# Static engine order in the attention, mixer operands split before DRAM, and PSUM sums in the FFN products of a hybrid block on one core

## The chip, the cores and the metric

The kernel runs on one core of one Trainium2 chip. The metric is the device time of one execution in microseconds (us). TensorE (PE) does the matmuls, VectorE (DVE) and ScalarE (ACT) everything on elements, GpSimd (POOL) a few memsets, and SyncE (SP) issues all DMAs, from one queue, in order.

## The reference, cut to what matters

One layer with 1024 tokens, 1024 channels, hidden width 2816, float32 throughout:

```python
u = modulate(rmsnorm(h, g_ff1), sh1, sc1)
h = h + 0.5 * gt1 * swiglu(u, w1_gate, w1_up, w1_down)
u = modulate(rmsnorm(h, g_mix), sh2, sc2)
qa, ka, va, xm, o_pre, ga, gb = split(u @ w_in)
ya = diff_attention(qa, ka, va, lam, g_subln)      # 8 heads x 2 score maps, chunk-causal
yb = mlstm_branch(xm, o_pre, ...)                  # conv, 4 heads, gated scan over chunks
h = h + gt2 * ((sigmoid(ga) * (ya @ w_proj_a) + sigmoid(gb) * (yb @ w_proj_b)) @ w_out)
u = modulate(rmsnorm(h, g_ff2), sh3, sc3)
h = h + 0.5 * gt3 * swiglu(u, w2_gate, w2_up, w2_down)
out = rmsnorm(h, g_final)
```

The modulation vectors come from `silu(c) @ w_ada + b_ada`, nine blocks of 1024 columns. In the attention every block of 128 queries has two softmaxes over its keys, whose difference multiplies v.

## The kernel before

**Precision.** A float32 product is made of three TensorE passes over rounded halves: operand = high part (`hi`, type fp32r) + low part (`lo`, the rest), and `mm3` (L130) does hi x hi, hi x lo, lo x hi into one PSUM bank (L132, L133, L134). So every operand is split once: a copy to `hi` on ACT and a subtraction to `lo` on DVE (`unit` L121 for weights, `split` L135, and `split_in` L140 for what has been loaded into the place of its low part).

**Stages, in order of time.** The first FFN (`ffn`), whose gate/up part does 3 hidden tiles plainly and 19 in steps of `gate_up`, then its down part; `stage_in`, which projects xm and the output gate, does the causal conv and the gate pre-activations; `stage_mlstm`; `stage_attn`; the merge; the second FFN; the final norm. The hidden layers and what the mixers read pass through DRAM.

**FFN.** `gate_up` (L385) uses one level of Strassen's scheme in Winograd's form: seven products instead of eight for a gate tile and an up tile, each product 4 x 3 matmuls of 128x512 into a PSUM bank of its own (`product`, 8 banks in the ring `psg`). One ACT copy and seven DVE additions then build the four outputs, and DVE also makes the weight combinations s1 to s4 (L391 to L397).

**stage_in.** `conv` (L728) copies the projection of channel tile j to `xp`, makes the conv in `acc` (L738, L741), Silu (L743), and splits both into the four tiles `xh` (one buffer each), which the tiny gate matmuls `gps` (L754, L756) read. It stores `acc` (L746) and `xp` (L747) to DRAM. The gate matmuls of tile j stand four projections later in TensorE's order; so the split of tile j+1 waits for the gate matmuls of tile j. Meanwhile `ada` (L114, L115) takes the columns of `w_ada` for later modulation vectors one by one: a 512 KB load, a multiply-and-sum on DVE.

**Sequence mixers.** mLSTM and attention are short dependent chains; dense projections (`job_qk`, `job_v`, `job_g`, `job_b`, cut into pieces of six matmuls by `chunk` L1003) fill TensorE between their steps. For attention, a head's block pair j does four score blocks (`sc`, L1276/L1277), softmax on DVE and ACT (L1278 to L1291), then for each pair of key blocks a turn (`pt`, four transposes, L1305; one buffer), its split into `ah` (ACT, L137) and `al` (DVE, L138), and the value products (`po`); at a head's end, the norm (`oss`, L1345).

**What orders the work.** TensorE's order is the source order, throughout (`manual_schedule(engines={PE})`, L1433). In the mixers `paced` (L1013) sorts items (due time, cost, function) by due times that `stage_attn` works out from fixed fractions of a block's length, and puts dense pieces between them. ACT and DVE are ordered by a scheduler with priorities; the items of `paced` get a head start of a fixed offset over the dense work's evictions:

```python
for due, cost, fn in sorted(items, key=lambda x: x[0]):
    while now < due:
        c = self.chunk()
        now = now + c if c else due
    with self.tc.high_priority(offset=self.ahead):
        fn()
```

A head's q and k are loaded from DRAM as one float32 tensor (`load`, L1240), then split: `Kh` on ACT (L143), `Kl` on DVE (L144), and for `Q`, whose low part lies on the upper 64 partitions, in four pieces. v is loaded and split the same way (`load_v`).

Of the kernel before, what the change touches and what calls it, by code (L numbers as in the profile page):

```python
# [15 lines left out]
PE = mybir.EngineType.PE  # L16
LNEXP = "natural_log_exp_and_others"
# [3 lines left out]
P = 128  # L21
# [18 lines left out]
class Halves:  # L40
    """two tiles with half of the tokens each"""
# [8 lines left out]

class Net:
    def __init__(self, ctx, tc, aps, dbg):
# [8 lines left out]
        self.uid = 0  # L61
        c = self.const
# [29 lines left out]
    # conditioning: one column block of w_ada per call  # L92
# [27 lines left out]
    # weights  # L120
# [9 lines left out]
    def mm3(self, ps, w, x, start, stop):  # L130
        nc = self.nc
        nc.tensor.matmul(ps, w[0], x[0], start=start, stop=False)  # L132
        nc.tensor.matmul(ps, w[0], x[1], start=False, stop=False)  # L133
        nc.tensor.matmul(ps, w[1], x[0], start=False, stop=stop)  # L134
# [22 lines left out]
    def rstd_of(self, ps, n, last):  # L157
        """1 / sqrt(ps / n + eps); `last`: the activation before it"""
# [9 lines left out]
    # 1 / rms over channels, on every partition, for some of the tokens  # L168
# [35 lines left out]
    def sum_square(self, n, i, m):  # L204
        """add channel tile m of half n, its i-th, to the running sum of squares"""
# [18 lines left out]
    def norm_step(self, i, q, j, bank):  # L224
        """first half's modulation behind the steps of the last products"""
# [8 lines left out]
    def norm_behind(self, i, n, m, bank):  # L234
        """behind the update of channel tile m of half n: statistics, and the first half's modulation"""
# [12 lines left out]
    def group(self, srcs, psp, tag, hook):  # L248
        """several M-tiles of a projection of u at once, channel tile by channel tile"""
# [15 lines left out]
    def ffn(self, wgu, wd, gt, first, plain, hid, after, step, extra=None):  # L265
        """h += gate * (silu(u w_gate) * (u w_up)) w_down; hidden passes through DRAM"""
# [33 lines left out]
    # The hidden layer goes to DRAM as the operands that down() takes: even tiles are its rows b1., odd ones b2.  # L300
# [9 lines left out]
    def store_right(self, hid, f, c2):  # L310
        """what follows from the second token half of tile f"""
# [8 lines left out]
    def store_left(self, hid, f, c1):  # L320
        """what follows from the first token half, behind store_right"""
# [10 lines left out]
    # One level of Strassen's scheme in Winograd's form: 7 products for the 8 of two tiles of w^T u, with  # L332
    # w^T = [a11 a12; a21 a22] (tiles x channel halves) and u = [b11 b12; b21 b22] (channel x token halves)
# [10 lines left out]
    def combine_u(self, x, pool):  # L344
        """t1 = b12 - b11, t2 = b22 - t1, -t4 = b21 - t2 for one channel tile of each half"""
# [26 lines left out]
    def gate_up(self, src, psg, rp, hid, f, first):  # L372
# [24 lines left out]
        A["s4"], A["s3"], A["a22"] = op(a12), op(s3), op(a22)  # L397
# [5 lines left out]
        def product(a, b):  # L403
            ps = psg.tile([P, NW], F32, name=self.nm("gu"), tag="gu")
            (h, l), u = A[a], B[b]
            for x in range(4):
                xs = slice(x * P, x * P + P)
                self.mm3(ps, (h[:, xs], l[:, xs]), u[x], x == 0, x == 3)
            return ps

        def plus(a, b):
            t = self.t512()
            add(t, a, b)
            return t

        m1 = self.t512()
        nc.scalar.copy(m1, product("a11", "b11"))
        c11 = plus(m1, product("a12", "b21"))
        if first:
            for x in range(4):  # L420
                self.combine_u3(x)
        nc.scalar.activation(c11, c11, AF.Silu)
# [4 lines left out]
        nc.scalar.activation(c12, c12, AF.Silu)  # L427
        m7 = product("s3", "t3")
        add(u4, u4, m7)
        nc.vector.tensor_mul(c12, c12, u4)  # L430
        self.store_right(hid, f, c12)
        add(m1, m1, m7)
        add(m1, m1, product("a22", "t4"))
        nc.vector.tensor_mul(c11, c11, m1)
        self.store_left(hid, f, c11)
# [66 lines left out]
        # product: its operands, weights to fetch meanwhile, a combination that takes a weight's place  # L502
# [43 lines left out]
    def first_start(self, srcs, psg, gtag, psd, dtag):  # L546
        """the first block's input: statistics, modulation and the first tiles as x and w_ada come in"""
# [42 lines left out]
    def first_norm(self, i, srcs, psg, gtag, psd, dtag):  # L590
        """later blocks' input: the first tiles run on one half while the other is normalised"""
# [8 lines left out]
    def out_tail(self, n, i, m, bank):  # L600
        """final norm behind the last update of h"""
# [36 lines left out]
    # one M-tile of a projection of u: PSUM halves  # L638
# [18 lines left out]
    def mix_setup(self):  # L657
# [8 lines left out]
        self.xcd, self.xmd, self.od, self.ybd = ([sc(f"{c}{h}", [P, 2, T]) for h in range(4)]  # L666
# [915 lines left out]
```

## Time and profile before

| | |
|---|---|
| median of 3 runs | 2679.71 us (2675.5 to 2680.58) |
| span of the profiled execution | 2681.1 us; the page gives no other time of it |
| TensorE busy | 2592.6 us, 97% |
| VectorE busy | 1877.3 us, 70% |
| ScalarE busy | 1288.3 us, 48% |
| DMA moved | 380.47 MB, mean 142 GB/s |

Stages by the profile: start 0 to 75 us, first FFN gate/up 75 to 467, its down part 467 to 694, `stage_in` 694 to 895, mLSTM 895 to 1211, attention and the dense work left after it 1211 to 1848, merge 1848 to 2035, second FFN 2035 to 2668, last norm and stores to 2681.

How to read it: busy times are instruction spans. Matmuls overlap, so a 128x512 matmul shows some 390 ns though one starts every 0.227 us (391.23 us for 1725 of them in the first gate/up part). PEclk is the clock that TensorE was granted, 1.00 for its higher level (2.4 GHz), 0.50 for the lower (1.2 GHz).

### The profile page before, as it was taken

What the parts mean: (1) busy time and instruction counts of PE and PEld (TensorE: products, weight loads), DVE (VectorE), ACT (ScalarE), POOL (GpSimd) and SP (SyncE); (2) the same over time, 40 slices, a digit from 0 to 9 for tenths busy, and PEclk for the clock granted to TensorE, in tenths of its full rate; (3) what the DMA queues carried; (4) which work ended last, traced back from release to release, by engine and by line L of the source; (5) the groups of instructions that cost most, each with busy time, mean ns of one, the idle gap of its engine ahead of it and who ended that gap; (6) DMA issues with size and microseconds to landing.
All of it is one profiled execution on the core that took longest, in us unless ns stands there. A gap on an engine that the chain in (4) does not pass through costs nothing.

```text
span 2681.1 us, 35203 instructions
## 1 busy us (share of the span) xinstructions
PE 2592.6 (97%) x12704; PEld 2155.8 (80%) x12704; DVE 1877.3 (70%) x3352; ACT 1288.3 (48%) x2369; POOL 22.5 (1%) x85
## 2 busy tenths in 40 slices
PE   6999999999899999999999999999999999999998
PEld 4888887778777799997777778777887888888886
DVE  7987878678795456646766766654467776766867
ACT  6333333446435366654666766753345332323444
POOL 0000000000000000000000000000000000000000
PEclk8999999999999999999999999999999999999999
DMA  7434345833674423334333333558342333236533
GB/s 262 162 130 145 118 149 185 274 99 104 215 258 149 140 91 118 111 100 121 111 102 106 99 105 115 159 198 277 131 140 87 110 98 115 99 102 216 161 95 122
DMA packets 174471, 380.47 MB, mean 142 GB/s; under 512 B 18405, under 2 KB 47529, under 8 KB 174297
## 3 DMA queue, kind: packets, MB, share of 16 engines
q1 hardware_dynamic: 174296, 378.24, 43.6%
q8 instruction: 99, 1.62, 0.2%
q14 instruction: 76, 0.61, 0.1%
HBM read 280.27 MB, written 97.90 MB: 141 GB/s over the span
## 4 chain that ended last, share of the span: by engine, by line
PE 84%; DMA 7%; DVE 5%; ACT 3%; issue 1%; SPq 0%; DVEq 0%; ACTq 0%; POOL 0%; POOLq 0%
PE gu L134 10%; PE gu L133 10%; PE gu L132 10%; PE acc L132 5%; PE acc L133 5%; PE acc L134 5%; PE ab L132 2%; PE ab L133 2%; PE ab L134 2%; PE dn L134 2%; PE dn L132 2%; PE dn L133 2%; PE gp L132 2%; PE gp L134 2%; PE gp L133 2%; PE pt L1305 1%
## 5 line engine op out<-in xcount | busy, mean ns | idle before, releaser
L132 PE MATMUL gu<-uh,wh 128*128 128x512 f32 x800 | 314.2, 393 | 10.1 <-ACT uh L201 8.8
L133 PE MATMUL gu<-ul,wh 128*128 128x512 f32 x800 | 313.4, 392 | 1.3 <-DVE ul L202 1.3
L134 PE MATMUL gu<-uh,wl 128*128 128x512 f32 x800 | 313.2, 391 | 0.8 <-DVE wl L127 0.7
L137 ACT CAST wh<-wr 128x512 fp32r<-128x512 f32 x228 | 134.0, 619 | 253.0 <-PE gu L133 194.0
L132 PE MATMUL acc<-uh,wh 128*128 128x512 f32 x616 | 241.9, 393 | 1.3 <-ACT uh L137 1.3
L133 PE MATMUL acc<-ul,wh 128*128 128x512 f32 x616 | 240.3, 390 | 1.3 <-DVE ul L138 1.3
L134 PE MATMUL acc<-uh,wl 128*128 128x512 f32 x616 | 239.8, 389 | 0.0
L126 ACT CAST wh<-wr 128x1024 fp32r<-128x1024 f32 x120 | 125.8, 1049 | 148.0 <-PE wo L133 46.1
L127 DVE TENSOR_TENSOR wl<-wr,wh 128x1024 fp32r<-128x1024 f32 x120 | 146.5, 1221 | 71.8 <-ACT wh L126 70.9
L132 PEld LDWEIGHTS gu<-uh,wh 128*128 128x128 f32 x800 | 151.2, 189 | 44.3 <-ACT uh L201 10.4
L133 PEld LDWEIGHTS gu<-ul,wh 128*128 128x128 f32 x800 | 151.2, 189 | 34.4 <-DVE ul L202 2.3
L134 PEld LDWEIGHTS gu<-uh,wl 128*128 128x128 f32 x800 | 151.1, 189 | 33.4 <-DVE wl L127 2.3
L133 PE MATMUL gu<-ut,wh 128*128 128x512 f32 x456 | 177.5, 389 | 0.0
L132 PE MATMUL gu<-ut,wh 128*128 128x512 f32 x456 | 177.4, 389 | 0.0
L134 PE MATMUL gu<-ut,wl 128*128 128x512 f32 x456 | 177.4, 389 | 0.0
L138 DVE TENSOR_TENSOR wl<-wr,wh 128x512 fp32r<-128x512 f32 x228 | 152.8, 685 | 1.6 <-ACT wh L137 1.6
L137 ACT CAST uh<-hr 128x512 fp32r<-128x512 f32 x154 | 95.4, 619 | 100.2 <-PE acc L134 63.6
L132 PEld LDWEIGHTS acc<-uh,wh 128*128 128x128 f32 x616 | 115.6, 188 | 28.6 <-ACT uh L137 2.5
L133 PEld LDWEIGHTS acc<-ul,wh 128*128 128x128 f32 x616 | 115.6, 188 | 26.3 <-DVE ul L138 2.2
L134 PEld LDWEIGHTS acc<-uh,wl 128*128 128x128 f32 x616 | 115.6, 188 | 24.1
L138 DVE TENSOR_TENSOR ul<-hr,uh 128x512 fp32r<-128x512 f32 x154 | 105.8, 687 | 35.5 <-ACT uh L137 35.0
L1281 ACT ACTIVATE p<-sc,lr 128x256 f32<-128x256 f32 (+7 forms) x128 | 94.8, 741 | 74.0 <-DVE lr L1279 72.1
(335 smaller groups left out, 6561.4 us busy)
## 6 DMA issues: line engine op xcount, KB each, us to landing
ada<-wada SPq DMA_DIRECT2D x72, 512.0 KB
wr<-win SPq DMA_DIRECT2D x48, 512.0 KB
wr<-w1gu SPq DMA_DIRECT2D x44, 512.0 KB
wr<-w2gu SPq DMA_DIRECT2D x44, 512.0 KB
wr<-wab SPq DMA_DIRECT2D x32, 512.0 KB
g<-t SPq DMA_DIRECT2D x32, 256.0 KB
t<-g SPq DMA_DIRECT2D x32, 256.0 KB
wr<-wout SPq DMA_DIRECT2D x16, 512.0 KB
```

The source lines that it names most:

```text
L126: nc.scalar.copy(hi, raw)
L127: nc.vector.tensor_sub(lo, raw, hi.bitcast(F32))
L132: nc.tensor.matmul(ps, w[0], x[0], start=start, stop=False)
L133: nc.tensor.matmul(ps, w[0], x[1], start=False, stop=False)
L134: nc.tensor.matmul(ps, w[1], x[0], start=False, stop=stop)
L137: (eng or self.nc.scalar).copy(hi, src)
L138: self.nc.vector.tensor_sub(lo, src, hi.bitcast(F32))
L1281: nc.scalar.activation(pc[c][:, 0:W], ps[:, 0:W], AF.Exp, bias=lr[:, 2 + c:3 + c], accum_out=lr[:, c:c + 1])
L1305: nc.tensor.transpose(pt[:, kk, i], a[i][:, kb * P:kb * P + P], self.ident)
```

## The change

No matmul is added or removed. Four parts:

1. **Attention order.** A class `Flow` takes the place of `paced` in `stage_attn`. Scores, values, outputs and loads of a head are generators that yield steps (engine, cost, function), take and give tokens for buffers, and wait for flags. `Flow.run` keeps a clock: a TensorE step that is ready is emitted, otherwise a piece of dense work. Inside it `manual_schedule(engines={PE, ACT, DVE})` holds, so ACT and DVE follow the source order as well. Weights of the dense work are fetched and split one job ahead (`unit_ahead`), evictions of dense banks are put into the model at a delay (`defer`). `p0` gets 6 buffers (was 4), `lr` 6 (was 4), `whl` 4 (was 3); `keep` goes from 90 to 45.
2. **Operands split before DRAM.** q, k, v, xc and xm are written as a high and a low tensor each and loaded as they are; the splits after the loads go, splits ahead of the stores come (in `rotate`, `job_v`), and for xc and xm the tiles `xh` themselves are stored.
3. **FFN sums in PSUM** (`seven`): x = a11*b11, copied by ACT, then s2*t2 and s3*t3 accumulate in the same bank, each copied by ACT; y = s1*t1, read by a DVE addition, then s4*b22 accumulates in it. Four banks instead of seven for a step, four DVE additions instead of seven, three ACT copies instead of one. The order of the seven products changes.
4. `dynamic_dma_scratch_size=1024` is passed at the build.

```diff
+class Flow:
+    LAT, MARGIN = 0.15, 0.4
...
+    def run(self):
+        while self.live:
+            while self.heap and self.heap[0][0] <= self.now:
...
+                    fn()
+                    self.free[eng] = max(self.free[eng], t) + cost
+                    self.push(self.free[eng] + self.LAT, gen)
+            if self.pe:
+                gen, _, cost, fn = self.pe.pop(0)
+                fn()
+                self.now += cost
+                self.push(self.now + self.LAT, gen)
+                continue
+            c = self.chunk()
...
-        self.whl = e(tc.tile_pool(name="whl", bufs=3))
+        self.whl = e(tc.tile_pool(name="whl", bufs=4))
...
-        m1 = self.t512()
-        nc.scalar.copy(m1, product("a11", "b11"))
-        c11 = plus(m1, product("a12", "b21"))
...
-        add(m1, m1, product("s2", "t2"))
-        u4 = plus(m1, product("s1", "t1"))
-        c12 = self.hidden_tile(f, 1)
-        add(c12, u4, product("s4", "b22"))
...
-        m7 = product("s3", "t3")
-        add(u4, u4, m7)
...
-        add(m1, m1, m7)
-        add(m1, m1, product("a22", "t4"))
+        x = product("a11", "b11")
+        c11 = kept(x)
+        add(c11, c11, product("a12", "b21"))
...
+        u2 = kept(product("s2", "t2", x))
+        y = product("s1", "t1")
+        u3 = kept(product("s3", "t3", x))
+        c22 = self.t512()
+        add(c22, u3, y)
+        out(1, 1, c22)
+        z = product("a22", "t4")
+        product("s4", "b22", y)
+        c12 = place() if place else self.t512()
+        add(c12, u2, y)
...
             nc.sync.dma_start(out=self.xcd[j // 2][:, j % 2], in_=acc)
-            nc.sync.dma_start(out=self.xmd[j // 2][:, j % 2], in_=xp[:, 4:4 + T])
+            for p in range(2):
+                nc.sync.dma_start(out=self.xcs[j // 2][p][:, j % 2], in_=xh[p].bitcast(F32))
+                nc.sync.dma_start(out=self.xms[j // 2][p][:, j % 2], in_=xh[2 + p].bitcast(F32))
...
+            for r in range(2):
+                rows = slice(64 * r, 64 * r + 64)
+                for dst, o in ((qs, src[0][r]), (kh, src[1][0]), (kl, src[1][1])):
+                    nc.sync.dma_start(out=dst[rows, :, part].bitcast(F32), in_=o)
...
+            with tc.manual_schedule(engines={PE, ACT, DVE}):
+                self.flow = flow
+                flow.run()
+                self.flow = None
```

`kept(ps)` copies a bank to a tile on ACT; `out` applies Silu or multiplies and stores. (`add` and `sub` are DVE operations.)

**DVE in the attention, around a turn of the first head**: `al` is the low part of a turn, `lr` the row maxima, and `t`/`qa` (after: `ro`) the rotation of a dense projection's result. Before:

```order
L1278 MEMSET sc_12290 64x64
L1279 TENSOR_REDUCE lr_12289<-sc_12290 128x1
L938 TENSOR_TENSOR t_12306<-qa_12179,cos 128x512
L939 TENSOR_TENSOR t_12307<-t_12305,sin 128x512
L941 TENSOR_TENSOR qa_12179<-qa_12179,sin 128x512
L940 TENSOR_TENSOR t_12306<-t_12306,t_12307 128x512
L1278 MEMSET sc_12324 64x64
L942 TENSOR_TENSOR t_12305<-t_12305,cos 128x512
L1279 TENSOR_REDUCE lr_12289<-sc_12324 128x1
L138 TENSOR_TENSOR al_12344<-pt_12338,ah_12343 128x512
```

And in the change, at the first head's second turn:

```order
L1118 TENSOR_TENSOR ro_12179<-ro_12179,ro_12176 128x512
L1119 TENSOR_TENSOR ro_12177<-ro_12177,ro_12178 128x512
L1112 TENSOR_TENSOR ro_12229<-qa_12124,cos 128x512
L1566 TENSOR_TENSOR al_12268<-pt_12237,ah_12256 128x512
L1501 MEMSET sc_12263 64x64
L1502 TENSOR_REDUCE lr_12233<-sc_12263 128x1
L1113 TENSOR_TENSOR ro_12230<-ro_12228,sin 128x512
L1121 TENSOR_TENSOR ro_12179<-ro_12179,ro_12180 128x512
```

Before, `al` stands behind the rotation's operations and the maximum of a later score block; in the change it stands ahead of that block's memset and maximum.

**DVE at the start of stage_in**: `wl` is the low part of the weight of the fourth xm projection, `ada` a column block of `w_ada`, `acc` the conv of the first tile. Before:

```order
L115 SCALAR_TENSOR_TENSOR ada_7128,mod_94<-ada_7128,crep_6282 128x1024
L117 TENSOR_TENSOR mod_94<-mod_94,vec 128x1
L115 SCALAR_TENSOR_TENSOR ada_7132,mod_94<-ada_7132,crep_6282 128x1024
L117 TENSOR_TENSOR mod_94<-mod_94,vec 128x1
L115 SCALAR_TENSOR_TENSOR ada_7136,mod_94<-ada_7136,crep_6282 128x1024
L127 TENSOR_TENSOR wl_6347<-wr_6344,wh_6346 128x1024
L738 TENSOR_SCALAR acc_6292<-xp_6284,vec 128x1024
```

And in the change, where the next eight `ada` (L213) follow only later:

```order
L225 TENSOR_TENSOR wl_6022<-wr_6019,wh_6021 128x1024
L332 TENSOR_TENSOR t_5994<-t_5981,t_5994 128x512
L225 TENSOR_TENSOR wl_6323<-wr_6320,wh_6322 128x1024
L320 TENSOR_TENSOR t_6073<-h_391,t_6060 128x512
L320 TENSOR_TENSOR t_6078<-h_392,t_6060 128x512
```

The fourth `wl` moves from behind the `ada` operations to right behind the third one.

**SP later in stage_in, its DMAs for channel tiles 4 to 6**: `xc`, `xm` and their `h` and `l` forms are stores, `wr` and `ada` loads, each of 512 KB. Before:

```order
L747 DMA xm_307<-xp_6484 128x1024
L114 DMA ada_7297<-wada 128x1024
L114 DMA ada_7362<-wada 128x1024
L746 DMA xc_303<-acc_6492 128x1024
L114 DMA ada_7367<-wada 128x1024
L124 DMA wr_7148<-win 128x1024
L114 DMA ada_7372<-wada 128x1024
L747 DMA xm_307<-xp_6568 128x1024
```

And in the change:

```order
L890 DMA xc_303<-acc_6558 128x1024
L212 DMA ada_7273<-wada 128x1024
L892 DMA xch_317<-xh_6465 128x1024
L893 DMA xmh_325<-xh_6467 128x1024
L892 DMA xcl_318<-xh_6466 128x1024
L893 DMA xml_326<-xh_6468 128x1024
L892 DMA xch_317<-xh_6552 128x1024
L893 DMA xmh_325<-xh_6554 128x1024
L892 DMA xcl_318<-xh_6553 128x1024
L893 DMA xml_326<-xh_6555 128x1024
L890 DMA xc_304<-acc_6645 128x1024
```

One store `xm` gives way to four stores of the tiles `xh`; the `ada` loads between them become few.

## Rows read from the trace of the kernel before

**Rows 1.** The page: span, and the chain that ended last by engine.

```profile
span 2681.1 us, 35203 instructions
...
PE 84%; DMA 7%; DVE 5%; ACT 3%; issue 1%; SPq 0%; DVEq 0%; ACTq 0%; POOL 0%; POOLq 0%
```

**Rows 2.** Stretches: length, busy us (instructions) by engine, PEclk, DMA share, GB/s.

```profile
75.00:467.00 392.00, 391.23 (x1725) 323.30 (x1724) 321.84 (x555) 125.56 (x212) 0.00 (x0) 1.00 0.44 146
694.00:895.00 201.00, 193.66 (x834) 151.64 (x834) 132.99 (x247) 85.02 (x110) 1.10 (x12) 0.98 0.55 190
895.00:1211.00 316.00, 306.17 (x2378) 293.09 (x2378) 184.01 (x469) 191.47 (x549) 13.94 (x32) 1.00 0.36 114
1211.00:1848.00 637.00, 604.87 (x3018) 498.90 (x3016) 418.33 (x770) 400.60 (x715) 6.49 (x32) 0.99 0.44 135
2035.00:2453.00 418.00, 417.63 (x1843) 345.49 (x1842) 306.10 (x491) 141.33 (x236) 0.00 (x0) 1.00 0.33 108
```

**Rows 3.** PE's waits, 1211 to 1848: total us, times, longest us; eleven rows.

```profile
PE pt L1305 <- DVE al L138: 9.2, 9, 2.2
PE sc L1277 <- DVE Kl L144: 3.1, 7, 0.7
PE sc L1276 <- DVE Q L144: 2.5, 1, 2.5
PE po L133 <- DVE al L138: 2.2, 3, 1.8
PE sc L1276 <- ACT Kh L143: 2.0, 4, 1.1
...
PE oss L1345 <- ACT t L1338: 0.6, 1, 0.6
```

**Rows 4.** The timeline around one such wait: start us, duration us, then [idle before].

```profile
1256.30 0.58 ACT L137 CAST ah<-pt 128x512 fp32r<-128x512 f32 x1
...
1259.17 0.67 DVE L138 TENSOR_TENSOR al<-pt,ah 128x512 fp32r<-128x512 f32 x1
1259.90 0.66 PE L1305 MATMUL pt<-ident,p 128*128 128x128 f32 x4 [1.40 <-DVE al L138]
```

**Rows 5.** Stretches at the lower clock, columns as in rows 2.

```profile
733.40:740.20 6.80, 4.79 (x11) 3.80 (x12) 6.80 (x8) 0.00 (x0) 0.00 (x0) 0.50 0.86 278
1453.60:1460.40 6.80, 5.47 (x15) 4.54 (x16) 5.39 (x11) 3.31 (x8) 0.00 (x0) 0.50 0.44 94
1566.30:1569.70 3.40, 3.36 (x11) 2.98 (x12) 3.14 (x6) 1.15 (x3) 0.00 (x0) 0.50 0.47 154
1747.20:1750.60 3.40, 3.40 (x9) 2.63 (x8) 2.85 (x6) 2.75 (x6) 0.00 (x0) 0.50 0.69 239
1846.20:1853.00 6.80, 4.37 (x10) 3.47 (x11) 5.84 (x9) 4.17 (x7) 0.00 (x0) 0.50 0.90 299
```

**Rows 6.** stage_in: PE's wait in 726 to 742, and DVE's timeline ahead of it.

```profile
PE dn L134 <- DVE wl L127: 5.4, 1, 5.4
...
732.98 1.23 DVE L115 SCALAR_TENSOR_TENSOR ada<-ada,crep 128x1024 f32<-128x1024 f32 x1 [1.87 <-DMA ada<-wada]
734.13 1.22 DVE L127 TENSOR_TENSOR wl<-wr,wh 128x1024 fp32r<-128x1024 f32 x1
```

**Rows 7.** stage_in: gate matmuls of tiles 3 to 7 (first and last start), and splits.

```profile
L754 PE MATMUL gps<-xh,G x20: 388/397/398, 797.4 to 828.3; 128*16 128x512 f32 x20
...
L138 DVE TENSOR_TENSOR xh<-xp,xh 128x1024 fp32r<-128x1024 f32 x8 | 9.8, 1220 | 0.0
```

**Rows 8.** Waits, columns as in rows 3: PE in the mLSTM, DVE in 2035 to 2453.

```profile
PE vps L1084 <- DVE mv L138: 3.3, 3, 1.8
...
DVE wr L391 <- DMA wr<-w2gu: 24.8, 17, 2.0
```

**Rows 9.** First gate/up part, by line: busy us, mean ns; idle time before and its releaser.

```profile
L413 DVE TENSOR_TENSOR t<-t,gu 128x512 f32<-128x512 f32 x38 | 26.0, 684 | 23.1 <-PE gu L134 14.7 <-issue 8.4
L417 ACT COPY t<-gu 128x512 f32<-128x512 f32 x19 | 11.2, 588 | 30.9 <-PE gu L134 30.9
```

More of the change, by code (lines that the diff above doesn't have):

```diff
@@ L1 @@
+import heapq
 from contextlib import ExitStack
@@ L16 @@
 PE = mybir.EngineType.PE
+DVE = mybir.EngineType.DVE
+ACT = mybir.EngineType.Activation
 LNEXP = "natural_log_exp_and_others"
@@ L370, in combine_u3, with seven @@
         self.split(t, *self.u_quarter(x, 0, 1))
-    def gate_up(self, src, psg, rp, hid, f, first):
+    def seven(self, src, bank, rp, out, first=False, place=None):
         nc = self.nc
@@ L401, in gate_up, with product @@
         B["t3"] = [self.u_quarter(x, 0, 1) for x in range(4)]
-        def product(a, b):
-            ps = psg.tile([P, NW], F32, name=self.nm("gu"), tag="gu")
+        def product(a, b, ps=None):
+            begin = ps is None
+            if begin:
+                ps = bank()
             (h, l), u = A[a], B[b]
@@ new lines, in load_v, with loads, sc_time @@
+                heads[hd] = v
+            def loads(hd):
+                if hd:
+                    yield "need", ("scored", hd - 1)
+                load(hd, slice(0, 256))
+                load(hd, slice(256, T))
+                yield "wait", 3.5
+                yield "set", ("qk", hd)
+                if hd:
+                    yield "need", ("valued", hd - 1)
+                load_v(hd)
+                yield "wait", 3.5
+                yield "set", ("v", hd)
+            def sc_time(W):
+                return sum(2 * {512: 0.227, 384: 0.174, 256: 0.12, 128: 0.112}[min(NW, W - o)] for o in range(0, W, NW))
@@ L1273, in item, with score, dots @@
+            def score(hd, j, i, c, a):
+                qb = 2 * j + i
+                W = qb * P + P
+                yield "need", ("qk", hd)
+                if hd or j or i or c:
+                    yield "need", ("begun", *self.prev[hd, j, i, c])
+                yield "take", "sc"
+                yield "set", ("begun", hd, j, i, c)
+                x = {}
+                def dots():
+                    x["ps"] = ps = psA.tile([P, T], F32, name=self.nm("sc"), tag="sc")
                     for o in range(0, W, NW):
@@ new lines, in score, with values, turn, high @@
+                yield "give", "p1"
+                yield "set", ("p", hd, j, i)
+            def values(hd, j, a):
+                nk = 2 * j + 2
+                if hd or j:
+                    yield "need", ("turned", *((hd, j - 1) if j else (hd - 1, 3)))
+                for i in range(2):
+                    yield "need", ("p", hd, j, i)
+                parts = {}
+                flow.spawn(flow.now, outputs(hd, j, parts))
+                for kp in range(nk // 2):
+                    yield "take", "pt"
+                    yield "take", "ah"
+                    x = {}
+                    def turn():
+                        x["pt"] = pt = psT.tile([P, 2, 2, P], F32, name=self.nm("pt"), tag="pt")
+                        for kk in range(2):
+                            for i in range(2):
+                                kb = 2 * kp + kk
+                                nc.tensor.transpose(pt[:, kk, i], a[i][0][:, kb * P:kb * P + P], self.ident)
+                    def high():
+                        x["h"] = a2.tile([P, 2, 256], F32R, name=self.nm("ah"), tag="ah")
+                        nc.scalar.copy(x["h"].rearrange("p k q -> p (k q)"), x["pt"].rearrange("p k i q -> p (k i q)"))
+                    def low():
+                        l = a2.tile([P, 2, 256], F32R, name=self.nm("al"), tag="al")
+                        nc.vector.tensor_sub(l.rearrange("p k q -> p (k q)"), x["pt"].rearrange("p k i q -> p (k i q)"),
+                                             x["h"].rearrange("p k q -> p (k q)").bitcast(F32))
+                        parts[kp] = x["h"], l
+                    yield "P", 0.44, turn
+                    if kp == nk // 2 - 1:
+                        yield "give", "p0"
+                        yield "give", "p0"
+                        yield "set", ("turned", hd, j)
+                    yield "A", 0.6, high
+                    yield "D", 0.69, low
+                    yield "give", "pt"
+                    yield "set", ("part", hd, j, kp)
@@ L1355, in stage_attn @@
+            own = lambda j: 2 * (sc_time(2 * j * P + P) + sc_time(2 * j * P + 2 * P)) + (j + 1) * (0.44 + 0.72)
+            items = [(hd, j, i, c) for hd in range(8) for j in range(4) for i in range(2) for c in range(2)]
+            self.prev = {b: a for a, b in zip(items, items[1:])}
+            t = 0.0
             for hd in range(8):
+                flow.spawn(0.0, loads(hd))
                 for j in range(4):
-                    a = [None, None]
-                    length = 4 * score_cost(j) + sum(c for c, _ in late) + dense / 32.0
@@ L1378, in stage_attn @@
-            for x, (cost, f) in enumerate(late):
-                put(off + 2.0 * x, cost, f)
-            put(off + 2.0 * len(late), 0.0, sq)
-            for x, (cost, f) in enumerate(norms):
-                put(off + 2.0 * len(late) + 3.0 * (x + 1), cost, f)
-            self.paced(items)
+                    a = {}
+                    length = own(j) + 0.43 + dense / 32.0
+                    for x in range(4):
+                        flow.spawn(t + x * length / 4, score(hd, j, x // 2, x % 2, a))
```

514 lines of the change are left out of this document (319 added, 195 removed).

## The prediction, as it was put on record

> **What bounds the kernel now.** I read the page first, for the span and the chain that ended last [rows 1]: 84% of 2681.1 us lies on TensorE. Then the stretches of the stages [rows 2], where the reader is to compare the length with PE's busy time: the gate/up parts leave 0.8 us of 392 and 0.4 us of 418, `stage_in` 7.3 of 201, the mLSTM 9.8 of 316, the attention with what follows it 32.1 of 637. Third, PE's waits there [rows 3]: eleven rows from 9.2 to 0.6 us, 26.7 in sum (most of the other 5.4 us lies at the end, ahead of the merge). Fourth, the clock: single stretches at 0.50 [rows 5], each behind a wait of about 2 us or more. Work done in 6.8 us at half clock takes 3.4 at full, so such a stretch costs half its length.
>
> So the kernel is as long as its matmuls, which the change leaves alone, and can only lose waits and lower clock. DVE or ACT work that goes is worth nothing where PE does not wait for it.
>
> **1. The order in the attention.** Of the 26.7 us, 9.2 are turns that wait for the `al` of the turn before, and 2.2 value products that wait for their own [rows 3]. The timeline shows why [rows 4]: `ah` ends at 1256.88, `al` (0.67 us) starts at 1259.17, because DVE does rotation work and a row maximum first; PE stands still for 1.40 us. The change puts `al` ahead of them, and in its TensorE order only one of the close pairs of turns (one dense piece, six matmuls, 1.36 us between them) is left of ten. A turn, `ah` and `al` need about 0.6 + 0.58 + 0.67 us and hand-overs. I take 9.5 of the 11.4 us as gone.
>
> `Kl`, `Kh` and `Q` cost 3.1, 2.0 and 2.5 us [rows 3]. Their splits go, but the loads stay: a head's keys have one buffer, so the loads still stand behind the last score of the head before, now with two tensors of k. I leave 0.3 us for each of seven heads and take 5.5 of 7.6 us as gone.
>
> The other six rows, 26.7 - 11.4 - 7.6 = 7.7 us, are softmax, norm and rotation hand-overs; the static order makes about half go, 4.
>
> The half-clock stretches of this part, 6.8 + 3.4 + 3.4 us [rows 5], cost 6.8 us. They stand behind the longest waits (those of rows 3 with 1.8 to 2.5 us); with these gone I take 5 as gone.
>
> New: near the end, when the dense pieces between are used up, scores and turns stand back to back and the next dense job waits for eight loads of 256 KB of the mLSTM's output, with their splits. No row shows it; the nearest is the wait of 5.4 us in [rows 6], and below it is nothing. I take 3.
>
> Sum: 9.5 + 5.5 + 4 + 5 - 3 = 21 us less. Its bounds are all waits and clock gone, 33.5, and, if the order only moves them, 0.
>
> **2. Operands split before DRAM, stage_in.** The fourth projection waits 5.4 us for its `wl` [rows 6]: DVE has `ada` operations ahead of it, which wait for their loads (1.87 us in the row). In the change, with the fourth buffer, `wl` stands ahead of the next eight `ada`, so the wait and the half-clock stretch behind it (3.4 of 6.8 us [rows 5]) go: 8.8 us less.
>
> Against it: the four `xh` tiles have one buffer, and are now read by four stores of 512 KB. The gates of tiles 3 to 7 start in 797.4 to 828.3 [rows 7], about 7.4 us apart, and the splits of a tile stand between two gates. The loop is now: gate about 1 us, two casts of 1.05, a last subtraction of 1.22, stores. How fast stores go: 299 GB/s at a share of 0.90 and 278 at 0.86 [rows 5] give about 330 at full share, so 4 x 0.524 MB take 6.4 us. If all of it is serial, a round takes 10.7 us, 3.3 too long; four rounds 13 us, and with a half-clock stretch each (1.7) 20. If only the bytes bind, the four stores with `xc` and a quarter of a load are 2.75 MB or 8.3 us, four rounds 4 us too long. The high parts are free earlier than the low ones, and `ada` loads between are fewer, so I am near the lower end: 4 us more. Bounds: 0 and 20.
>
> **3. mLSTM.** The splits of xm and xc behind the loads go (32 pairs), 64 halves are loaded instead of 32; rotation and v get splits ahead of their stores, as many. PE waits 9.8 us in 316 [rows 2], 3.3 of it for `mv`, a low part that DVE makes late [rows 8]. I take 2 us less; the bounds are -6 and, if the first loads come late, +4.
>
> **4. FFN sums in PSUM.** DVE loses 3 additions of 0.684 a step and ACT gains 2 copies of 0.588 [rows 9], 38 steps: 78 us less on DVE, 45 more on ACT. Both are covered by PE, which has no wait to give back [rows 2]. New are waits of PE for a bank: s4\*b22 may start only when the addition c22 has read y, and between s3\*t3 and s4\*b22 stands one product, 12 x 0.227 = 2.72 us. In it ACT's copy (0.59) and DVE's addition (0.68) must run, 1.27 us; ACT stands idle ahead of its copy now, released by PE [rows 9], so about 1.4 us are to spare. For x, the copy alone must come within the other products. I take 1 us more; below is 0, above is a rival.
>
> A rule speaks against this part. Rows of both gate/up parts show PEclk at 1.00 throughout [rows 2], with a bank for every product. The Trainium skill ("TensorE: Matmul & The Clock Gate", A second HAM failure mode: psum-queue depth-cycling) tells of a kernel in which PE idles briefly and often between groups as it cycles through PSUM banks, and whose clock falls back again and again. By the rows the sum holds 1 us for these parts; by that rule it would hold the price of the second rival.
>
> **Sum.** -21 - 8.8 + 4 - 2 + 1 = -27 us (-26.8). From the span of 2681.1 us that is 2654. The page gives no time of this execution besides the span; it lies 1.4 us above the median of the runs, within their spread of 5 us, so for a median I take 2653 us.
>
> **The rivals.**
>
> *The bank of y comes late (slower).* Mechanism: DVE follows its queue; where a load holds it, c22 waits and PE stands before s4\*b22. For it: DVE waits 24.8 us for weights in the second gate/up part, up to 2.0 us at a time [rows 8], and the spare is 1.4. Against it: these waits stand ahead of the next step's combinations, not just ahead of c22, and DVE is busy 322 of 392 us [rows 2], with less to do now. At 1 us a step it costs 38 us: 2653 - 1 + 38 = 2690. It turns the sign at 28 / 38 = 0.73 us a step. Chance 0.10.
>
> *The clock falls in the gate/up parts (slower).* If each step has a bank wait long enough to be followed by one stretch as in [rows 5], 3.4 us at half clock, 38 steps cost 38 x 1.7 = 65 us and the waits: over 2715. For it stands no row here; against it, the 1.4 us to spare, where the rows show the fall behind waits of about 2. That is the rule of the skill named above. Chance 0.04.
>
> *The stores hold up the gates.* The serial round of part 2: 20 us instead of 4, 2669. For it: the tiles have one buffer, and the share of the DMA engines is 0.55 in this stage already [rows 2]. Chance 0.14.
>
> *The order does not do what it says.* `Flow` orders ACT and DVE by a model; where a load is late, a queue in fixed order lets everything behind it wait, which the scheduler's order also did but with other neighbours. Then part 1 gives 0 and the sum is -6: 2674, and a little worse is within no change. Chance 0.12.
>
> *Nearly all waits go.* Parts 1 and 2 at their bounds: -33.5 - 8.8 - 2 = -44, 2635. Chance 0.08.
>
> **How the numbers follow.** My forecast has the rest, 0.52, and its own range is 2640 to 2668 (part 1 from 12 to 30 us). A measurement of this kernel tells 0.2% (5.4 us) from no change. Faster by more than that are the forecast, the last rival, nearly all of the third (0.12) and a third of the fourth (0.04): 0.76. No change: half of the fourth and a bit of the first and third, 0.09. Slower: 0.15, from the first, the second and the rest. The range reaches from 2632, under the best case, to 2690, the first rival's price.
>
> **What would show it.** Right: in 1211 to 1848 of the new trace the row of turns waiting for `al` falls under 2 us and no `Kl` row is left; the wait at the fourth xm projection is gone; gate matmuls wait a few us in sum; the two gate/up parts stay within 3 us of 392 and 418 with PEclk 1.00. Wrong: rows of `gu` waiting for a DVE addition in most steps; waits of `gps` for stores above 15 us; or attention waits of 20 us or more under other names.

## The result, and the profile after

The changed kernel takes **2697.85 us** (median of 4 runs, 2695.55 to 2700.98) beside 2680.14 us before (4 runs, 2675.5 to 2681.11): the ratio is **1.0069** with the interval 1.005 to 1.0088. The forecast was 2653 us, 1% faster. The sign was wrong, and the time lies above the range.

The page of the profiled execution (span 2698.3 us, before 2681.1 [rows 1]):

```profile
span 2698.3 us, 35191 instructions
...
PE 2593.2 (96%) x12704; PEld 2163.0 (80%) x12704; DVE 1789.7 (66%) x3214; ACT 1271.9 (47%) x2374; POOL 22.8 (1%) x85
...
PE 83%; DMA 8%; DVE 5%; ACT 2%; issue 1%; SPq 1%; POOL 0%; DVEq 0%; ACTq 0%; POOLq 0%
```

PE's busy time on the page of before was 2592.6 us. So the span of 17.2 us more is not work: PE stands still 105.1 us where it stood still 88.5. DVE was relieved as the diff says (1877.3 us before, 1789.7 now), and that does not show in the time.

Where the time went can be told from four marks that both traces have: the first matmul of `qp` (the projections of q and k that fill the mLSTM and the attention), the last of `po` (the attention's value product), the last of `ab` (the merge's projections) and the end. In the tile views of the changed kernel the last column is the first and last start:

```profile
L254 PE MATMUL qp<-uh,wh x256: 387/389/799, 885.3 to 1608.3; 128*128 128x512 f32 x128
L254 PE MATMUL po<-ah,av x160: 276/281/562, 1230.2 to 1798.2; 128*128 128x256 f32 x160
L254 PE MATMUL ab<-uh,wh x256: 387/389/799, 1758.0 to 2000.2; 128*128 128x512 f32 x128
```

From these rows and the same rows of the other kernels, in us (e1 to e6 are the experiments below; each column is one execution, and executions of one kernel lie up to 12 us apart, 2672.23 to 2684.36 us in 19 of the kernel before, so a few us in one column say little):

| stretch | before | after | e1 | e2 | e3 | e5 | e6 | forecast of the difference |
|---|---|---|---|---|---|---|---|---|
| start to first `qp` (FFN, `stage_in`) | 895.6 | 885.3 | 884.9 | 883.4 | 888.8 | 889.2 | 891.4 | -8.8 + 4 |
| first `qp` to last `po` (mLSTM, attention) | 882.4 | **912.9** | 884.7 | 891.0 | 865.4 | 901.0 | 858.6 | -21 - 2 |
| last `po` to last `ab` (rest of the merge) | 202.7 | 202.0 | 200.8 | 200.0 | 199.5 | 201.4 | 200.8 | 0 |
| last `ab` to the end (second FFN) | 700.4 | 698.1 | 698.2 | 698.1 | 698.8 | 698.8 | 698.8 | +1, with the first FFN |

Everything outside the mixers came as forecast or better. In the mixers 23 us were to go, and 30.5 us came. The windows, columns as in [rows 2], which they answer:

```profile
75.00:467.00 392.00, 391.52 (x1726) 323.56 (x1725) 294.13 (x500) 146.99 (x253) 0.00 (x0) 1.00 0.45 147
694.00:895.00 201.00, 200.30 (x877) 158.06 (x878) 136.41 (x251) 88.90 (x115) 1.10 (x12) 1.00 0.75 260
895.00:1211.00 316.00, 295.95 (x2319) 285.41 (x2317) 172.90 (x467) 169.57 (x508) 14.36 (x32) 0.98 0.48 152
1211.00:1848.00 637.00, 593.32 (x2970) 493.54 (x2971) 388.15 (x737) 356.08 (x670) 6.42 (x32) 0.97 0.53 156
2035.00:2453.00 418.00, 417.06 (x1838) 344.65 (x1838) 281.16 (x438) 164.71 (x276) 0.00 (x0) 1.00 0.30 100
```

The first, second and fifth are full at PEclk 1.00. In the third PE's idle time grew from 9.8 to 20.1 us and in the fourth from 32.1 to 43.7, and the clock fell in both. PE's waits there, as in [rows 3]:

```profile
PE pt L1558 <- DVE p L1520: 15.6, 2, 14.7
PE pt L1558 <- DVE al L1566: 12.5, 5, 2.8
PE qp L256 <- DVE wl L247: 9.2, 3, 8.4
PE po L254 <- ACT osb L1606: 4.7, 2, 3.1
```

The many small waits of before have become a few large ones. `Q` and `Kl` waiting for DVE are gone as forecast. The turns that wait for `al` are fewer (5, not 9) but longer (12.5 us, not 9.2), and a turn that waits for `p` costs 14.7 us at one place.

**What DVE itself waits for** answers it. DVE's waits from 1200 to 1760, rows in which a rotation waits for its own earlier stores:

```profile
DVE ro L1113 <- DMA qkl<-ro: 31.5, 7, 5.5
...
DVE ro L1113 <- DMA qkh<-ro: 13.5, 1, 13.5
```

With two smaller rows (L1115 3.9, L1112 1.7) that is 50.6 us; on ACT four such waits (L1120) make 21.6 us more. DVE of the kernel before has no such row, but its ACT waited for the rotation's stores already, 10.0 us in three rows, of which the first is

```profile
ACT qa L927 <- DMA qk<-qa: 5.7, 2, 3.3
```

The warning stood in the trace of before, though [rows 3] shows none of it, being waits of PE alone. `ro` is the ring of five tiles that `rotate` (L1103) takes at once. Before, a rotation sent two tensors from tiles of the larger ring `t512` and of its own; now it sends four from these five tiles. How one late store reaches PE is seen in the timeline (start, duration, then the idle time before it and what ended it):

```profile
1402.23 0.56 SPq L1108 DMA_DIRECT2D qkl<-ro  x1
1402.82 0.62 ACT L1120 CAST ro<-ro 128x512 fp32r<-128x512 f32 x1 [1.38 <-DVE ro L1112]
1403.93 0.58 ACT L1562 CAST ah<-pt 128x512 fp32r<-128x512 f32 x1 [0.48 <-PE pt L1558]
1408.41 0.69 DVE L1113 TENSOR_TENSOR ro<-ro,sin 128x512 f32<-128x512 f32 x1 [4.64 <-DMA qkl<-ro]
1409.02 0.69 DVE L1121 TENSOR_TENSOR ro<-ro,ro 128x512 fp32r<-128x512 f32 x1
1409.62 0.68 DVE L1566 TENSOR_TENSOR al<-pt,ah 128x512 fp32r<-128x512 f32 x1
1410.37 0.65 PE L1558 MATMUL pt<-ident,p 128*128 128x128 f32 x4 [2.29 <-DVE al L1566]
```

The second rotation of a pair needs for its `y` (L1113) a tile that the store issued at 1402.23 still reads; the row starts at 1408.41, 6.2 us after that issue. The order is fixed, so `al`, whose `ah` is done at 1404.51, stands behind it until 1409.62, and the next turn waits. L1121, the last step of the *first* rotation, was ready at 1403.44 and waits too, so its own store goes out late as well. The long wait of 14.7 us is the same thing at the change from one head to the next:

```profile
1279.03 0.62 SPq L1456 DMA_DIRECT2D Kh<-qkh  x1
...
1285.69 0.55 SPq L1108 DMA_DIRECT2D qkh<-ro  x1
1286.35 0.55 SPq L1108 DMA_DIRECT2D qkl<-ro  x1
1298.35 0.69 DVE L1113 TENSOR_TENSOR ro<-ro,sin 128x512 f32<-128x512 f32 x1 [13.48 <-DMA qkh<-ro]
1300.89 0.62 ACT L1120 CAST ro<-ro 128x512 fp32r<-128x512 f32 x1 [17.50 <-DMA qkl<-ro]
1302.76 1.28 DVE L1520 SCALAR_TENSOR_TENSOR p<-p,lr,p 128x1024 f32<-128x1024 f32 x1
1304.09 0.90 PE L1558 MATMUL pt<-ident,p 128*128 128x128 f32 x3 [14.66 <-DVE p L1520]
```

Ten loads of the next head's keys and queries go out from 1279.03 on, the two stores behind them, and the rows that wait for them start 12.7 and 14.5 us after their issues. These are two rotation steps, one on DVE and one on ACT, and the softmax of both engines stands behind.

Why a store lands so late the DMA view shows, in 40 slices of the stretch 1400 to 1412: busy share of the 16 DMA engines in tenths, and GB/s.

```profile
DMA  2222221089515130122122222222222221102413
GB/s 68 89 109 89 109 102 75 34 314 382 178 41 41 7 14 7 34 61 61 61 102 109 96 102 102 102 96 109 102 102 96 109 89 61 41 0 48 34 7 14
```

SP has issued nothing since 1402 but the two stores of 1402.23 and 1403.47, and from 1406 to 1409.6 they run at about 102 GB/s and a share of 0.2 to 0.3 (digit 2), where a slice at 1402.7 has 382. The four stores of a rotation, 4 x 0.262 MB, need 10.3 us at that rate. The trace of before has the same plateau, at 1256 to 1278, with two stores a rotation:

```profile
DMA  0000013222223322219786100321222232222100
GB/s 0 0 0 0 0 30 19 11 56 78 97 104 104 82 41 63 93 78 212 231 324 276 52 0 4 41 11 26 63 97 101 101 86 71 86 97 101 63 7 0
```

The store's target is walked as 4 x 32 x 512, and the Trainium skill ("DMA: Bandwidth & Descriptors", Rules for kernel authors) says that an access pattern whose outermost dimension counts c < 16 is confined to at most c of the engines. Four of 16 would be a share of 0.25: the rows agree.

### The profile page after: what moved, and what is told of

It reads as the page before. It is cut to its first block, busy times and chain, and to the rows that moved or that the text cites. A ratio compares the mean times of both kernels' runs of the same rounds, so it can differ in the third digit from the quotient of the medians.

```text
span 2698.3 us, 35191 instructions
## 1 busy us (share of the span) xinstructions
PE 2593.2 (96%) x12704; PEld 2163.0 (80%) x12704; DVE 1789.7 (66%) x3214; ACT 1271.9 (47%) x2374; POOL 22.8 (1%) x85
## 2 busy tenths in 40 slices
DMA packets 200966, 426.63 MB, mean 158 GB/s; under 512 B 20324, under 2 KB 63784, under 8 KB 200792
## 4 chain that ended last, share of the span: by engine, by line
PE 83%; DMA 8%; DVE 5%; ACT 2%; issue 1%; SPq 1%; POOL 0%; DVEq 0%; ACTq 0%; POOLq 0%
PE gu L254 10%; PE gu L255 10%; PE gu L256 10%; PE acc L254 5%; PE acc L255 5%; PE acc L256 5%; PE dn L254 2%; PE dn L255 2%; PE dn L256 2%; DMA qkl<-ro 2%; PE gp L254 2%; PE gp L255 2%; PE gp L256 2%; PE ab L256 2%; PE ab L254 2%; PE ab L255 2%
## 5 line engine op out<-in xcount | busy, mean ns | idle before, releaser
L224 ACT CAST wh<-wr 128x1024 fp32r<-128x1024 f32 x81 | 85.0, 1050 | 144.7 <-PE wo L255 46.0
L225 DVE TENSOR_TENSOR wl<-wr,wh 128x1024 fp32r<-128x1024 f32 x81 | 98.9, 1221 | 51.2 <-ACT wh L224 50.3
L539 ACT COPY t<-gu 128x512 f32<-128x512 f32 x114 | 66.7, 585 | 137.8 <-PE gu L256 134.0
```

The lines of the kernel that those rows point to most:

```text
L539: nc.scalar.copy(t, ps)
```

## The experiments

The theory: the ring of five `ro` tiles, held by four slow stores, delays the rotation, and a queue in fixed order hands each delay on to all that stands behind it. The rivals: the fixed order is bad by itself; the FFN's shared banks cost; the fourth weight buffer costs; the added traffic (426.63 MB beside 380.47) makes everything late. `dynamic_dma_scratch_size`, the change's fourth part, stands in every run here but e8 and was not tested alone.

**e1_stores4: the same stores, each as four transfers of 32 rows.**

```diff
-                nc.sync.dma_start(out=self.qkd[hd][p][:, :, h].rearrange("q c r t -> (q c) r t")[:, :, ns], in_=o)
+                for q in range(2):
+                    for c in range(2):
+                        r = 64 * q + 32 * c
+                        nc.sync.dma_start(out=self.qkd[hd][p][q, c, h][:, ns], in_=o[r:r + 32])
```

> The change, with each of the four stores of a rotation issued as four DMAs of 32 partitions. Theory A (the rotation's stores land late, its ring of five tiles is held by them, and the fixed order of VectorE and ScalarE lets everything behind wait): the stores land in under 4 us instead of 7 to 10, VectorE's waits of rotation rows for stores fall under 5 us in the attention, TensorE's wait of 14.7 us for p and the turns' waits of 2.2 to 2.8 us once per head go; 2665 to 2675 us. Rival B (the model's order itself is bad, whatever the stores do): the turns' waits stay, 2690 to 2700. Rival C (46 MB more DMA traffic makes everything late): no gain, 2695 to 2705.

Measured: 2665.86 us, ratio 0.9964 (0.9953 to 0.9975). Same bytes, same order, same ring, and 1.0% below the change. The DMA view at 1400 to 1412 now:

```profile
DMA  6000003673663745175373663644849800000000
GB/s 164 0 0 7 7 14 75 144 184 89 164 157 89 184 103 123 34 191 137 103 184 89 164 157 103 171 123 109 198 164 375 341 7 0 0 0 0 0 0 0
```

PE's and DVE's waits from 1200 to 1760:

```profile
PE pt L1561 <- DVE p L1523: 12.6, 2, 11.3
...
DVE ro L1116 <- DMA qkh<-ro: 12.1, 1, 12.1
DVE ro L1116 <- DMA qkl<-ro: 10.1, 6, 2.4
```

The turns at `al` are gone from the list; the one long wait is left, where the stores stand behind ten loads. The time is as expected, two of the signs are not: DVE's waits for stores were to fall under 5 us and are 22.2, and the wait for `p` was to go. So the stores' narrowness is one cause, and the ring still holds at one place.

**e2_free_order: the change, with ACT and DVE ordered by the scheduler again.** TensorE keeps its new order.

```diff
-            with tc.manual_schedule(engines={PE, ACT, DVE}):
+            with tc.manual_schedule(engines={PE}):
```

> The change, with TensorE alone in fixed order in the attention; VectorE and ScalarE are ordered by the scheduler as in the kernel before. Theory A and rival B: turns no longer stand behind a rotation that waits for its ring, TensorE's waits in the attention fall by more than 20 us; 2670 to 2682 us. Rival C: the waits stay, 2690 or more.

Measured: 2677.07 us, ratio 1.0005 (0.9993 to 1.0016). The fixed order costs 0.64% here (about 17 us). The rotation still waits for its stores, but less hangs on it:

```profile
PE pt L1558 <- DVE al L1566: 10.0, 8, 3.2
...
DVE ro L1113 <- DMA qkl<-ro: 17.7, 6, 4.3
```

With a row of 3.0 us (L1115) these waits are 20.7 us instead of 50.6, and the turn that waited 14.7 us for `p` is gone. The time is as expected; PE's waits from 1200 to 1810 fell by 17 us, not by more than 20 (48.1 to 30.7, all rows). So the fixed order costs, but turns go on waiting for `al` without it: the scheduler's order hands the ring's delay on too.

**e3_ring9: nine `ro` tiles, four stores as in the change.** The space for them comes from the weights: three buffers, as before the change.

```diff
-        self.whl = e(tc.tile_pool(name="whl", bufs=4))
+        self.whl = e(tc.tile_pool(name="whl", bufs=3))
...
-        b, x, y, z, w = (self.rope.tile([P, NW], F32, name=self.nm("ro"), tag="ro", bufs=5) for _ in range(5))
+        b, x, y, z, w = (self.rope.tile([P, NW], F32, name=self.nm("ro"), tag="ro", bufs=9) for _ in range(5))
```

> The change, with nine tiles in the rotation's ring instead of five; to make room the ring of split weights goes back from four buffers to three. Theory A: waits of rotation rows for stores nearly vanish, so the attention gains as in the run with four DMAs a store; three weight buffers give back some of the 10 us gained in stage_in; 2665 to 2685 us. Rivals B and C: 2698 or more.

Measured: **2656.19 us**, ratio 0.993 (0.9915 to 0.9945), better than the 2665 expected at the least, and 3 us from the forecast of 2653. That nearness is partly chance: by the table the mixers gave 17.0 us of the 23 forecast, and the stretches behind them 4.8 us that were not in the sum. In DVE's waits no `ro` row for a DMA is left, and PE's waits from 1200 to 1810 are:

```profile
PE qp L256 <- DVE wl L247: 8.6, 1, 8.6
PE po L254 <- ACT osb L1606: 3.9, 1, 3.9
PE pt L1558 <- DVE p L1520: 3.5, 1, 3.5
```

No row of turns waiting for `al`. The stores are issued as in the change; with tiles to spare no rotation step waits for them. The bytes moved are those of the change as well (426.63 MB), so the added traffic is not what made it slow.

**e5_three_weights: the change with three weight buffers and its ring of five**, the control for e3.

```diff
-        self.whl = e(tc.tile_pool(name="whl", bufs=4))
+        self.whl = e(tc.tile_pool(name="whl", bufs=3))
```

> The change with three buffers for split weights, as the kernel before has, and the rotation's ring of five tiles: the other half of the run with nine tiles. Theory A: the ring alone made the gain of 41 us there, so here the attention is as in the change; the fourth projection of stage_in waits again, by 3 to 5 us and its lower clock; 2698 to 2708 us. If the three buffers had a part in the gain: 2690 or less.

Measured: 2691.29 us, ratio 1.0047 (1.0032 to 1.0062), with the 14.3 us turn at `p` and six turns at `al` (12.5 us) as in the change. The time is below the 2698 to 2708 us expected, and the intervals of change and e5 overlap: what the fourth weight buffer costs lies between nothing and some 0.5% and is not settled. Beside e5, which has three as well, the ring alone is worth 1.0047 - 0.9930, or 1.2%, some 31 us.

**e4_old_ffn and e8_ffn_alone: the FFN's part taken out of the change, and put alone into the kernel before.** In e4 `gate_up` is the old one with a bank for every product; in e8 everything else is as before. The core of e4's diff (e8's is the same with the signs turned):

```diff
-    def seven(self, src, bank, rp, out, first=False, place=None):
+    def gate_up(self, src, psg, rp, hid, f, first):
...
-                self.mm3(ps, (h[:, xs], l[:, xs]), u[x], begin and x == 0, x == 3, True)
+                self.mm3(ps, (h[:, xs], l[:, xs]), u[x], x == 0, x == 3)
...
-            nc.scalar.copy(t, ps)
+            add(t, a, b)
```

> The change, with the FFN products of the kernel before (a bank for each product, seven additions). All theories: the gate/up parts have no wait either way, so the same within 3 us: 2695 to 2701.

> The kernel before with the FFN sums in PSUM alone. My forecast has 1 us more for this part, with 0 below and 38 or more by the rivals that make TensorE wait for a bank: 2675 to 2681 us if the spare of 1.4 us holds, 2710 or more if not.

Measured: e4 2693.22 us, 1.0076 (1.0057 to 1.0095), beside 1.0069 for the whole change; e8 2676.48 us, 0.999 (0.9978 to 1.0002). e4 lies 2 us below its expected range, e8 within it. Neither differs from its partner by what can be told here. The first gate/up part of e8 (in e4 it has PE 392.00 and DVE 322.92, PEclk 1.00):

```profile
75.00:467.00 392.00, 391.61 (x1727) 323.76 (x1726) 289.43 (x496) 145.84 (x254) 0.00 (x0) 1.00 0.44 147
```

33 us of DVE's work in this stretch alone come and go, and PE is full at PEclk 1.00 in both.

**e6_ring9_free: e3 with ACT and DVE ordered by the scheduler** (the edits of e3 and of e2).

> Nine tiles in the rotation's ring, three weight buffers, and the order of VectorE and ScalarE left to the scheduler in the attention. It tells what the fixed order is worth once the ring holds nothing up. Theory A with my forecast's term (turns wait for their low part about 10 us in sum without it, and some lower clock): turns wait 8 to 12 us, 2666 to 2676 us. If the fixed order is worth nothing by itself: 2653 to 2660.

Measured: **2648.71 us**, ratio 0.9888 (0.9865 to 0.991). PE's waits from 1200 to 1810:

```profile
PE sc L1495 <- ACT p L1507: 7.4, 1, 7.4
...
PE pt L1558 <- DVE al L1566: 0.4, 1, 0.4
```

The expectation failed: turns were to wait 8 to 12 us without the static order, 2666 to 2676 us. With the ring freed they need no static order on DVE and ACT. The row of 7.4 us is the wait at the start of the attention, which e7 is about, under another name.

**e7_ring9_first12: e3 with the first attention step 12 us later.** It was meant for the wait that stands at the start of the attention in every version of the change (8.4 us in the change, 8.6 in e3, 7.4 in e6). In the change it reads:

```profile
1208.85 0.88 DVE L1385 SCALAR_TENSOR_TENSOR hT<-t,vec,hT 128x256 f32<-128x256 f32 x2 [3.17 <-DMA t<-xc]
1213.29 0.29 DVE L1502 TENSOR_REDUCE lr<-sc 128x1 f32<-128x128 f32 x1 [2.83 <-DMA yb<-hT]
1213.94 1.21 DVE L247 TENSOR_TENSOR wl<-wr,wh 128x1024 fp32r<-128x1024 f32 x1
1215.20 0.79 PE L256 MATMUL qp<-uh,wl 128*128 128x512 f32 x1 [8.37 <-DVE wl L247]
```

The low part of a weight (`wl`) stands on DVE behind one of the mLSTM's last outputs, which waits for a load, and a row maximum, which waits for the store of that output.

```diff
-            t = 0.0
+            t = 12.0
```

> Nine tiles in the ring, three weight buffers, and the model's first score of the attention 12 us later, so that the low part of the first dense weight stands ahead of the row maxima of the first scores, which wait for a store of the mLSTM before. Theory A: the wait of 8.6 us at the start of the attention and its lower clock go; 2640 to 2650 us. If that wait has another cause (a late load of the weight): it stays, 2655 to 2660.

Measured: 2661.03 us, ratio 0.9937 (0.9918 to 0.9956), no better than e3; the expectation failed. The wait only took other names (another, 5.6 us, came at 1780 ahead of the merge, `ab` for `uh`):

```profile
PE qp L254 <- ACT wh L246: 9.1, 2, 7.7
```

**e9_ring9_free_stores4: e6 with the stores of e1.**

> Nine tiles in the ring, three weight buffers, VectorE and ScalarE ordered by the scheduler, and each rotation store as four DMAs. Theory A: with nine tiles no rotation row waits for a store any more, so that a faster landing adds nothing: within 4 us of the run without the four DMAs, 2645 to 2653 us. If the late landing also costs through the loads behind it on SyncE's queue: 2640 or less.

Measured: 2664.2 us, ratio 0.9952 (0.9937 to 0.9968): slower than e6, and the expectation failed. A row is new that e6 does not have:

```profile
PE qp L254 <- ACT wh L246: 5.3, 2, 2.9
```

That cast of a weight comes late. A store of four transfers takes mostly 1.7 to 1.8 us of SP's queue in e1's timeline, one of a single transfer 0.52 to 0.56 in the change's. 64 stores at 1.2 us more are about 77 us of the queue that also issues the weights' loads. e10, with four weight buffers and the same stores, has the row too (3.0 us). That the queue makes the weights late is argued, not shown; and the row explains 5.3 us of the 17 or so by which the ratios differ.

**e10_ring5_free_stores4: the change's ring of five and four weight buffers, e1's stores, scheduler's order.**

> The change (five tiles in the ring, four weight buffers) with VectorE and ScalarE ordered by the scheduler and each rotation store as four DMAs. Theory A: the two remedies add up in part, since each takes a side of the same wait: 2652 to 2664 us. If they are two separate losses that add in full (33 us and 21 us): 2644 or less.

Measured: 2657.38 us, ratio 0.9925 (0.9906 to 0.9944). With landing made fast, the ring of five costs little: 0.4% beside e6, with intervals that just meet. A larger ring or faster stores do the same job; together (e9) they are slower than the ring alone.

**e11_ring9_fixed_again and e12_ring9_free_again: e3 and e6 once more, on one chip, in five rounds**, for the price of the fixed order with the ring freed.

> Nine tiles in the ring, three weight buffers, fixed order of VectorE and ScalarE, on the same chip as the next run. Ratio to the kernel before 0.992 to 0.994. If the fixed order is worth nothing either way, the two runs have overlapping intervals; if it costs, this one is slower by 0.2% or more.

> The same with the order of VectorE and ScalarE left to the scheduler. Ratio 0.988 to 0.992 if the fixed order costs, 0.992 to 0.994 if it is worth nothing.

Measured: e11 2659.62 us, 0.994 (0.9925 to 0.9954); e12 **2647.49 us**, 0.9898 (0.9882 to 0.9915). The intervals don't meet: the fixed order of DVE and ACT costs 0.42%, about 11 us. Where these lie is only partly shown. The profiled executions differ by 6.6 us: from 1200 to 1220 PE is busy 9.8 us in e11 and 13.1 in e12, from 1220 to 1700 476.7 of 480 and 477.9; the rest lies in clock and single waits. This stays open.

Taken together the runs say more on the theory than each alone. Under the fixed order, nine tiles and three weight buffers bring 1.4% (the change against e3); under the scheduler's order they bring 1.2% (e2 against e6). The fixed order costs 0.6% with the short ring (e2), 0.4% with the long one (e11 against e12) and 0.4% with the split stores (e1 against e10). By these intervals the two costs simply add: that the fixed order makes the ring's delay worse is seen in single rows of the trace, but is not shown in the time.

e6 and e12, the change with nine rotation tiles, three weight buffers and the scheduler's order, is the best version run: about 1.0 to 1.1% below the kernel before.

## Why the prediction was wrong

**The step that failed** is one half sentence of part 3: "rotation and v get splits ahead of their stores, as many". Splits were counted, and stores and tiles were not. Nothing was charged for a ring of five tiles under four stores instead of two. In its place: 50.6 us of DVE waits for these stores from 1200 to 1760, four more on ACT (21.6 us, 17.5 of it ahead of 1300.89), and by e5 against e3 some 31 us of time. A second term had the wrong sign: part 1 took 4 us as won by the static order of DVE and ACT, and that order cost 11 us or more. Part 2 did price stores, those of `xh`, by the best rates of [rows 5] (278 and 299 GB/s, of loads and stores mixed); the same trace shows the rotation's stores at 95 to 105 GB/s, which the prediction did not use. Twice the bytes at that rate are 10.3 us a rotation instead of 5.1.

**Part 1, the order (-21).** The gain came once the ring was freed, and its reason was half wrong. Turns at `al` then wait 0.4 us or not at all, `Kl` and `Q` wait for DVE no more, and first `qp` to last `po` comes out 17.0 us (e3) and 23.8 us (e6) shorter than before, in second executions 15.8 (e11) and 19.4 (e12); the forecast for parts 1 and 3 together was 23. But e6 has no static order on DVE and ACT: what the step "the change puts `al` ahead of them" took for the cause is not needed. Whether TensorE's new order, the splits ahead of DRAM or the larger buffers (`p0`, `lr`) make the gain is not shown, as no run takes them apart. The static order costs 11 us (e11, e12), 17 with the short ring (e2). Not in the sum was the wait at the start of the attention (8.4 us): scores now start while DVE still waits for the mLSTM's last loads. The hole at the end came out near its price (3.1 us, 3 taken), but by luck: it stands at 1752, where value products wait for ACT to copy their bank (`osb`), and is not the wait of a dense job for the mLSTM's output that was priced.

**Part 2, `stage_in` (-8.8 + 4).** Right, and better: -10.3 us. The fourth projection's wait is gone, and the gates are not held up: their matmuls start from 749.4 to 818.6, the same 69 us from first to last as before (759.1 to 828.3), and that of each tile follows the last by about the 7.4 us of [rows 7]. So the third rival, stores hold up the gates, fell; of its 20 us nothing came, though the DMA share of the stage rose from 0.55 to 0.75.

**Part 3, mLSTM (-2; bounds -6 to +4).** Outside its bounds by the idle time of the window, 10.2 us more, of which 4.2 belong to the start of the attention. The longest wait here is one for `sch`, the high part of the mLSTM's weighted scores:

```profile
930.06 0.73 SPq L222 DMA_DIRECT2D wr<-wv  x1
940.51 1.04 ACT L224 CAST wh<-wr 128x1024 fp32r<-128x1024 f32 x1 [8.72 <-DMA wr<-wv]
941.92 0.58 PE L1344 MATMUL num<-mv,sch 128*128 128x258 f32 x1 [4.77 <-ACT sch L259]
```

ACT makes `sch` behind the cast of a dense weight, whose load was issued at 930.06 behind four stores of the first rotations and came 10 us later. That those stores made it late is not shown: e2, with the same ring and four weight buffers, has the wait too (4.3 us), e5, with the same ring and three, has not. This part stays open.

**Part 4, FFN (+1).** Right: 0 (e4, e8), with both gate/up stretches within 1 us of PE's full time. The first and second rivals fell with it. The rule that the prediction drew from the Trainium skill ("TensorE: Matmul & The Clock Gate", A second HAM failure mode: psum-queue depth-cycling) does not bite here: PEclk is 1.00 in both stretches, and PE's only waits for a bank in them are two of 0.2 us.

**The rivals.** Nearest came "the order does not do what it says", with its words "where a load is late, a queue in fixed order lets everything behind it wait". It was priced at a gain of 0 for part 1 and given 0.12; the late transfers were stores, not loads, and the short ring cost some 31 us (e3, e5). A fixed order was treated as one that can only fail to help. The list of signs that would prove the forecast wrong held the right one: attention waits of 20 us or more under other names (`p`, `wl` and `osb`, 29.5 us together).

## What to carry to other kernels

When a tile that was stored once is stored as two halves, count for each tile of its ring how long it is held: bytes over the rate at which *this* transfer runs in the trace, plus the transfers ahead of it on the queue. An engine's queue hands every late transfer on to all that stands behind it, whether the source or the scheduler made the order: the short ring cost about as much under either. Fix the order of the engines that do not bound the kernel only if a run shows that it pays; here it cost 0.4 to 0.6%. A ring of nine instead of five turned +0.5% (e5) into -0.7% (e3) here.

## What the runs showed of the hardware

A 256 KB store of 128 partitions to a target walked as 4 x 32 x 512 moved at about 102 GB/s with a share of 0.2 to 0.3; as four transfers of 32 rows it moved mostly at 75 to 198 GB/s in slices, at four times 0.43 us of issue on SP. 65.5 KB / 0.43 us is 152 GB/s, so the queue may now have set the pace; no run tests it. Behind the ten loads of a head, issued within 6.5 us, two such stores held their tiles for 12.7 and 14.5 us (issues at 1285.69 and 1286.35, the released rows at 1298.35 and 1300.89).
